# Decaying q on GpSimd so that the state's share of the output accumulates in PSUM, with the banks dealt anew and k's third buffer given up

## The chip, the core and the metric

The kernel runs on one NeuronCore of one Trainium2 chip. A core has five engines that run side by side, each with a queue of its own: TensorE (PE, with its weight loads shown apart as PEld), VectorE (DVE), ScalarE (ACT), GpSimd (POOL) and SyncE (SP, which here issues the transfers). They work on the on-chip memory SBUF; PE writes its sums to a second memory, PSUM, which this program divides into eight banks: two `pj`, two `a`, two `b`, one `c`, one `d`. The metric is the device time of one execution in microseconds (us), the median of some runs.

## What is computed

Two residual layers and a final RMS norm over 1024 tokens of width 1024: an even layer (dilated attention beside a gated recurrence) and an odd layer (gated delta rule). Only the odd layer is touched. Its core, per value head, cut to what matters:

```python
attn_qk = jnp.einsum('bhnid,bhnjd->bhnij', qc, kc) * decay
q_dec = qc * jnp.exp(gcum)[..., None]
k_tail = kc * jnp.exp(gcum[..., -1:] - gcum)[..., None]
g_last = jnp.exp(gcum[..., -1])

def step(state, inp):
    u_n, w_n, a_n, qd_n, kt_n, gl_n = inp
    v_new = u_n - jnp.einsum('bhcd,bhdv->bhcv', w_n, state)
    o = jnp.einsum('bhcd,bhdv->bhcv', qd_n, state) + jnp.einsum('bhij,bhjv->bhiv', a_n, v_new)
    new_state = state * gl_n[..., None, None] + jnp.einsum('bhcd,bhcv->bhdv', kt_n, v_new)
    return new_state, o
```

`q` and `k` come out of a projection, a causal convolution over four tokens and SiLU, and are normalised; `v` likewise without the norm. Sixteen value heads share eight key heads, two to one. The output `o` is the sum of two parts: the decayed `q` against the state of the chunks before, and the chunk's own attention against its new values.

## The kernel before

The odd layer works through eight key heads, `hh` 0 to 7, with two value heads `e` each. The 1024 tokens are eight chunks of 128. For each head there are four pieces of work, written as Python generators, each `yield` giving a number that says how much other work is to be written behind it.

- `proj(j)` is filling work for PE. From head 2 on it first writes `way_out(j-2)`, the gate projection `oz` in four halves of 24 matmuls; then `conv` for k of head j+1, for the two value heads of head j (`v..0`, `v..1`), and for q of head j, each in two halves of 512 tokens and 24 matmuls (lines 143 to 145). A half's sums go from one of two `pj` banks by ACT into `ub`, which has one buffer (line 822); ACT writes the first product into the destination tile (line 825), DVE adds three (line 827), ACT takes tanh into `ub` (line 830) and DVE finishes (line 831). The destination of k is `kT`, from `k_tile`, with three buffers; that of q is `q`, with two; that of a value head is `cv`, with one.
- `invert(hh)` inverts the lower triangular matrices of head hh: `kk` into bank `c` (line 986), a long chain on DVE (lines 1004 to 1009), and small matmuls from bank `c` in turn, `qp`, `up`, `q2`, `u2` (lines 1030 to 1061).
- `recur(hh)` walks the eight chunks. For chunk c: `ks` = k against the state (line 1105, bank `b`), `r` on DVE (line 1108), `qs` = q against the state (line 1111, bank `d`), its decay by ACT into `oq` (line 1114), `vp` (line 1120, bank `d`), `vt` on DVE and `vn` on ACT from it, `kv` (line 1129, bank `b`), the new state `S` on DVE (line 1133), `op` = attention against `vn` (line 1140, bank `b`), the next chunk's `qk` (line 1091, bank `d`), and on DVE the sum of `op` and `oq` into `bv` (line 1143), which ACT squares (line 1148). Bank `d` has one buffer, `b` two. `decay_a(c)` loads the decays of a chunk into `gca`, GpSimd adds the causal mask (line 1079) and ACT takes two exponentials (line 1081); this is done one chunk ahead.
- `normed` and `gated` finish a head: GpSimd scales `bv` (line 928), PE transposes it (line 935).

The three loops are woven together while the program is written: `mix(recur(hh), fill, 2.8)` with `fill = blend(invert(hh+1), proj(hh+1), 0.8)`. So while head hh is in its recurrence, head hh+1 is inverted and k of head hh+2 is convolved. Going through the numbers that the generators yield, from head 2 on the four `oz` halves are written by chunk 2, k's two halves beside chunk 4's `ks` and `vp`, the first value head's halves beside chunk 5 and chunk 6's `ks`, the second value head's beside chunks 6 and 7, and q's at the end.

The written order is a priority, not the order in the queues: the tile framework deals the instructions to the engines when it builds the program, a tile's first write waiting until the slot it takes has been given up by its last reader. What is then in an engine's queue runs in that order. The attention of the even layer alone has PE's order fixed by hand.

At the last head the filling work is the output projection; `y_parts(0)` takes two `kT` slots and two of `kn` for its first operands.

Of the kernel before, what the change touches and what calls it, by code (L numbers as in the profile page):

```python
# [9 lines left out]
F32 = mybir.dt.float32  # L10
F32R = mybir.dt.float32r
BF16 = mybir.dt.bfloat16
I32 = mybir.dt.int32
AF = mybir.ActivationFunctionType
ALU = mybir.AluOpType
# [3 lines left out]
P = 128  # L19
D = 1024  # L20
T = 1024
# [57 lines left out]
def trunk_kernel(ctx: ExitStack, tc: tile.TileContext, x, ew, ewo, ow, owab, owo, nw, fnw, lbl, hnw,  # L79
                 cw, dtb, alog, onw, cst, out):  # L80
    nc = tc.nc
    dve, act, pe, pool = nc.vector, nc.scalar, nc.tensor, nc.gpsimd
# [8 lines left out]
    def bank(tag, shape, name):  # L91
        return pp.tile(shape, F32, name=name, tag=tag, bufs=BANKS[tag])
# [647 lines left out]
    def odd_layer(es):  # L740
        sp = es.enter_context(tc.tile_pool(name="od", bufs=1))
        gt = {n: sp.tile([P, NT, 16], F32, name=f"g_{n}") for n in ("beta", "gc", "ngc", "eg", "nbeg", "etl", "egl")}
# [70 lines left out]
        KT, KN, SC, Q, BV, CQ, SS, VT, US = {}, {}, {}, {}, {}, {}, {}, {}, {}  # L813
# [32 lines left out]


        def k_tile(j):
            KT[j] = sp.tile([P, T], F32, name=f"kT{j}", tag="kT", bufs=3)
            return KT[j]  # L850

        def q_tile(j):
# [108 lines left out]
        def decays(hh, c, w):  # L961
            g = sp.tile([P, 2, 128], F32, name=f"gc{w}{hh}_{c}", tag=f"gc{w}", bufs=2)
            nc.sync.dma_start(g, bass.AP(tensor=gcd.tensor, offset=gcd.offset + (c * 16 + 2 * hh) * 128,
                                         ap=[[0, P], [128, 2], [1, 128]]))
            return g

        def invert(hh):
            kT = KT[hh]
# [4 lines left out]
            def decay_l(c):  # L973
                gcB = decays(hh, c, "l")

                for e in range(2):
                    act.activation(gcB[:, e, :], gcB[:, e, :], AF.Relu, bias=gt["ngc"][:, c, 2 * hh + e:2 * hh + e + 1])
                act.activation(gcB, gcB, AF.Exp, scale=-1.0)
                return gcB

            ahead_l = [decay_l(0)]
            for h in range(2):
                kk = bank("c", [P, 4, 128], f"kk{hh}_{h}")
                for c in range(4 * h, 4 * h + 4):
                    k_ = kT[:, c * 128:(c + 1) * 128]
                    pe.matmul(kk[:, c - 4 * h, :], k_, k_, start=True, stop=True)
                for c in range(4 * h, 4 * h + 4):
                    gcB = ahead_l.pop()
                    if c < NT - 1:
                        ahead_l.append(decay_l(c + 1))  # L990
                    for e in range(2):
                        dve.scalar_tensor_tensor(L[:, 2 * c + e, :], kk[:, c - 4 * h, :], SC[hh][:, 0, c, e:e + 1],
                                                 gcB[:, e, :], op0=ALU.mult, op1=ALU.mult)
                yield (15 if h else 7.0), 0.9


            for b in range(4):
# [32 lines left out]
                    pe.matmul(qp[a0[r], u, :], L[b0[r], u, a0[r]], Un[b0[r], u, :], start=True, stop=True)  # L1030
            act.copy(Q_[a0[0], :, 0:32], qp[a0[0]])
            dve.tensor_copy(Q_[a0[1], :, 0:32], qp[a0[1]])
            yield 1.5, 1.3
            up = bank("c", [P, 16, 32], f"up{hh}")
            for u in range(16):
                for r in range(2):
# [8 lines left out]
                r = slice(32 * b, 32 * b + 32)  # L1045
                pool.tensor_copy(U[r, :, r], Un[r])

            yield 2.0, 1.8
            for h in range(2):

                q2 = bank("c", [P, 4, 64], f"q2{hh}_{h}")
                for u in range(8 * h, 8 * h + 8):
                    pe.matmul(q2[u % 2 * 64:u % 2 * 64 + 64, u // 2 % 4, :], L[64:128, u, 0:64], U[64:128, u, 64:128],
                              start=True, stop=True)
# [3 lines left out]
            for h in range(2):  # L1058
# [3 lines left out]
                for e in range(2):  # L1062
                    d = U[0:64, 8 * h + e:8 * h + 8:2, 64:128]
# [8 lines left out]
        def recur(hh):  # L1072

            kT, kn, q, bv, U = KT[hh], KN[hh], Q[hh], BV[hh], US[hh]
            ss = SS[hh] = sp.tile([P, NT, 2], F32, name=f"oss{hh}", tag="oss", bufs=2)

            def decay_a(c):
                DA = decays(hh, c, "a")
                pool.tensor_tensor(DA, DA, MA[:, None, :].to_broadcast([P, 2, 128]), op=ALU.add)
                for e in range(2):  # L1080
                    act.activation(DA[:, e, :], DA[:, e, :], AF.Exp, bias=gt["ngc"][:, c, 2 * hh + e:2 * hh + e + 1])
                return DA

            def attend(c):

                DA = ahead_a.pop()
                if c < NT - 1:
                    ahead_a.append(decay_a(c + 1))
                qk = bank("d", [P, 128], f"qk{hh}_{c}")
                s = slice(c * 128, (c + 1) * 128)  # L1090
                pe.matmul(qk, kT[:, s], q[:, s], start=True, stop=True)
                A = sp.tile([P, 2, 128], F32, name=f"A{hh}_{c}", tag="A", bufs=2)
                dve.tensor_tensor(A, qk[:, None, :].to_broadcast([P, 2, 128]), DA, op=ALU.mult)
                return A

            ahead_a = [decay_a(0)]
            yield 1.0
            A = attend(0)
            St = None
            for c in range(NT):  # L1100
                col = [slice(2 * hh + e, 2 * hh + e + 1) for e in range(2)]
                s = slice(c * 128, (c + 1) * 128)
                if c:
                    ks = bank("b", [P, 2, 128], f"ks{hh}_{c}")
                    pe.matmul(ks, kT[:, s], St, start=True, stop=True)
                    r_ = sp.tile([P, 2, 128], F32, name=f"r{hh}_{c}", tag="r")
                    for e in range(2):
                        dve.scalar_tensor_tensor(r_[:, e, :], ks[:, e, :], SC[hh][:, 1, c, e:e + 1],
                                                 bv[:, c, e, :], op0=ALU.mult, op1=ALU.add)
                    qs = bank("d", [P, 2, 128], f"qs{hh}_{c}")  # L1110
                    pe.matmul(qs, q[:, s], St, start=True, stop=True)
                    oq = sp.tile([P, 2, 128], F32, name=f"oq{hh}_{c}", tag="oq")
                    for e in range(2):
                        act.activation(oq[:, e, :], qs[:, e, :], AF.Copy, scale=gt["eg"][:, c, col[e]])
                else:
                    r_ = bv[:, 0]
                yield 1.0
                vp = bank("d", [P, 2, 128], f"vp{hh}_{c}")
                for e in range(2):
                    pe.matmul(vp[:, e, :], U[:, 2 * c + e, :], r_[:, e, :], start=True, stop=True)  # L1120
                if c < NT - 1:
                    vt = sp.tile([P, 2, 128], F32, name=f"vt{hh}_{c}", tag="vt")
                    dve.tensor_tensor(vt, vp, gt["etl"][:, c, 2 * hh:2 * hh + 2, None].to_broadcast([P, 2, 128]), op=ALU.mult)
                vn = sp.tile([P, 2, 128], F32, name=f"vn{hh}_{c}", tag="vn")
                act.copy(vn, vp)
                yield 1.0
                if c < NT - 1:
                    kv = bank("b", [P, 2, 128], f"kv{hh}_{c}")
                    pe.matmul(kv, kn[:, c, :], vt, start=True, stop=True)
                    Sn = sp.tile([P, 2, 128], F32, name=f"S{hh}_{c}", tag="S", bufs=2)  # L1130
                    if c:
                        for e in range(2):
                            dve.scalar_tensor_tensor(Sn[:, e, :], St[:, e, :], gt["egl"][:, c, col[e]],
                                                     kv[:, e, :], op0=ALU.mult, op1=ALU.add)
                    else:
                        dve.tensor_copy(Sn, kv)
                    St = Sn
                op = bank("b", [P, 2, 128], f"op{hh}_{c}")
                for e in range(2):
                    pe.matmul(op[:, e, :], A[:, e, :], vn[:, e, :], start=True, stop=True)  # L1140
                A = attend(c + 1) if c < NT - 1 else None
                if c:
                    dve.tensor_tensor(bv[:, c], op, oq, op=ALU.add)
                else:
                    dve.tensor_copy(bv[:, c], op)
                for e in range(2):
                    jk = sp.tile([P, 128], BF16, name=f"oj{hh}_{c}_{e}", tag="jk", bufs=2)
                    act.activation(jk, bv[:, c, e, :], AF.Square, accum_out=ss[:, c, e:e + 1])
                yield 1.0
# [8 lines left out]
        def y_parts(g):  # L1158
            if g:
                return y_load(*y_tile(f"lo{g % 2}", 8 + g), g * 256)  # L1160
            yh = [sp.tile([P, T], F32R, name=f"oyh{c}", tag="kT", bufs=3) for c in range(2)]
            yl = [sp.tile([P, T], F32R, name=f"oyl{c}", tag="kn", bufs=3) for c in range(2)]
            y_load(yh, yl, 0)
            for t in range(NT):
                nc.sync.dma_start(hres(t), h1[t * 128:(t + 1) * 128, :])
            return yh, yl
# [103 lines left out]
```

## Time and profile before

| what | us |
|---|---|
| median of three runs | 2290.05 (2288.1 to 2291.62) |
| the profiled execution, its own time | 2290.27 |
| its span, first to last instruction | 2288.5 |
| recurrence, first `ks` to last `ks` | 1342.5 to 2122.2 |
| PE busy from 1340 to 2045, sum of the rows of the windows | 644 of 705 |
| DVE busy in the same stretch | 556 |
| ACT busy in the same stretch | 394 |

A row of a group names the line, the engine, the operation, the output and inputs by the program's names, the count, then the busy time and the mean of one in ns, then the engine's idle time ahead of them and who ended it. A row of the waits names who waited for whom, the sum in us, how often, and the longest. A matmul on float32 appears as two instructions. In the windows each engine's busy time in a stretch is followed by its count of instructions. Matmul ends are modelled and some records are missing, so PE's busy time is a guide and the distance from one start to the next is the better measure of its pace.

### The profile page before, as it was taken

What the parts mean: (1) busy time and instruction counts of PE and PEld (TensorE: products, weight loads), DVE (VectorE), ACT (ScalarE), POOL (GpSimd) and SP (SyncE); (2) the same over time, 40 slices, a digit from 0 to 9 for tenths busy, and PEclk for the clock granted to TensorE, in tenths of its full rate; (3) what the DMA queues carried; (4) which work ended last, traced back from release to release, by engine and by line L of the source; (5) the groups of instructions that cost most, each with busy time, mean ns of one, the idle gap of its engine ahead of it and who ended that gap; (6) DMA issues with size and microseconds to landing.
All of it is one profiled execution on the core that took longest, in us unless ns stands there. A gap on an engine that the chain in (4) does not pass through costs nothing. (4 is left out here: it accounts for less than half of the span.)

```text
span 2288.5 us, 54642 instructions
## 1 busy us (share of the span) xinstructions
PE 2171.9 (95%) x22597; PEld 1809.0 (79%) x22597; DVE 1427.0 (62%) x3364; ACT 963.4 (42%) x2623; POOL 226.5 (10%) x236
## 2 busy tenths in 40 slices
PE   7999999999999999988999988989899989899998
PEld 6888888898888888866887776767777767678787
DVE  6444444444444444456777887878788877855777
ACT  5333333333333332322236663755555555544223
POOL 0000000000000000000000012131212121210000
PEclk9999999999999999999999998999999999999999
DMA  4111111113222323352323221121212121214232
GB/s 145 38 48 48 44 47 48 43 39 95 78 82 84 90 83 92 97 160 88 102 97 104 59 56 62 53 79 46 76 43 76 52 74 59 65 60 148 91 113 109
DMA packets 101864, 175.83 MB, mean 77 GB/s; under 512 B 16752, under 2 KB 34032, under 8 KB 101616
## 3 DMA queue, kind: packets, MB, share of 16 engines
q1 hardware_dynamic: 101616, 172.35, 24.2%
q8 instruction: 177, 2.90, 0.5%
q14 instruction: 71, 0.58, 0.1%
HBM read 127.07 MB, written 25.23 MB: 67 GB/s over the span
## 5 line engine op out<-in xcount | busy, mean ns | idle before, releaser
L113 DVE TENSOR_TENSOR w_lo<-raww,w_hi 128x512 fp32r<-128x512 f32 x292 | 211.9, 727 | 151.1 <-ACT w_hi L112 147.1
L112 ACT CAST w_hi<-raww 128x512 fp32r<-128x512 f32 x292 | 181.1, 620 | 270.1 <-PE op L145 68.0
L143 PE MATMUL av<-w_hi,hn_hi 128*128 128x256 f32 x512 | 149.0, 291 | 0.0
L143 PE MATMUL bi<-w_hi,hn_hi 128*128 128x256 f32 x512 | 147.0, 287 | 0.0
L144 PE MATMUL bi<-w_lo,hn_hi 128*128 128x256 f32 x512 | 145.3, 284 | 0.0
L144 PE MATMUL av<-w_lo,hn_hi 128*128 128x256 f32 x512 | 144.8, 283 | 0.0
L145 PE MATMUL bi<-w_hi,hn_lo 128*128 128x256 f32 x512 | 144.8, 283 | 0.0
L145 PE MATMUL av<-w_hi,hn_lo 128*128 128x256 f32 x512 | 144.7, 283 | 0.0
L575 ACT ACTIVATE P<-P,nm 128x256 f32<-128x256 f32 (+7 forms) x128 | 71.4, 559 | 130.2 <-DVE nm L573 130.0
L143 PE MATMUL op<-w_hi,yplo 128*128 128x512 f32 x288 | 113.5, 394 | 1.6 <-DVE hr L273 0.9
L145 PE MATMUL op<-w_hi,yplo 128*128 128x512 f32 x288 | 112.2, 390 | 0.0
L144 PE MATMUL op<-w_lo,yplo 128*128 128x512 f32 x288 | 112.1, 389 | 0.0
L143 PE MATMUL pv<-hn_hi,w_hi 128*128 128x512 f32 x256 | 107.0, 418 | 2.6 <-ACT uv L822 2.6
L143 PE MATMUL oz<-hn_hi,w_hi 128*128 128x512 f32 x256 | 109.4, 427 | 0.0
L273 DVE TENSOR_TENSOR hr<-hr,op 128x512 f32<-128x512 f32 x128 | 86.1, 684 | 34.5 <-PE op L145 34.0
L145 PE MATMUL pv<-hn_hi,w_lo 128*128 128x512 f32 x256 | 104.3, 407 | 0.0
L144 PE MATMUL pv<-hn_lo,w_hi 128*128 128x512 f32 x256 | 102.6, 401 | 0.0
L144 PE MATMUL oz<-hn_lo,w_hi 128*128 128x512 f32 x256 | 102.3, 400 | 0.0
L145 PE MATMUL oz<-hn_hi,w_lo 128*128 128x512 f32 x256 | 102.0, 398 | 0.0
L581 DVE STREAM_TRANSPOSE PB<-P 128x256 f32<-128x256 f32 (+3 forms) x64 | 54.6, 854 | 74.9 <-ACT P L575 74.8
L143 PEld LDWEIGHTS av<-w_hi,hn_hi 128*128 128x128 f32 x512 | 97.9, 191 | 3.5 <-issue 1.9
L144 PEld LDWEIGHTS bi<-w_lo,hn_hi 128*128 128x128 f32 x512 | 98.1, 192 | 0.0
(354 smaller groups left out, 6044.9 us busy)
## 6 DMA issues: line engine op xcount, KB each, us to landing
raww<-in_ew_dram SPq DMA_DIRECT2D x128, 256.0 KB, 3.1
raww<-in_ow_dram SPq DMA_DIRECT2D x100, 256.0 KB, 3.0
V<-v SPq DMA_DIRECT2D x256, 64.0 KB, 2.0
rawy<-ymix SPq DMA_DIRECT2D x64, 256.0 KB, 2.7
raww<-in_ewo_dram SPq DMA_DIRECT2D x32, 256.0 KB, 3.0
gcl<-gcd SPq DMA_DIRECT2D x64, 128.0 KB, 3.0
gca<-gcd SPq DMA_DIRECT2D x64, 128.0 KB, 3.0
ymix<-oy SPq DMA_DIRECT2D x32, 256.0 KB, 2.0
```

Source lines behind the costliest of these rows:

```text
L112: act.copy(hi, raw)
L113: dve.tensor_tensor(lo, raw, hi.bitcast(F32), op=ALU.subtract)
L143: pe.matmul(ps, lh, rh, start=start, stop=False)
L144: pe.matmul(ps, lh, rl, start=False, stop=False)
L145: pe.matmul(ps, ll, rh, start=False, stop=stop)
L273: dve.tensor_tensor(dst[:, n], src[:, n], ps, op=ALU.add)
L575: act.activation(Pm[:, e, w0:], Pm[:, e, w0:], AF.Exp, bias=nmx[:, e:e + 1], scale=0.125, accum_out=den[:, i, e:e + 1])
L581: dve.transpose(PB[:, :, i * WG + w0:(i + 1) * WG], Pm[:, :, w0:])
```

## The change

- `decay_a(c)` also makes, from chunk 1 on, `qe`: ACT takes the exponential of the raw decays for both value heads in one instruction of 128x256, and GpSimd multiplies it with q. This stands ahead of the mask's addition on the same tile. `qe` has two buffers of 1 KB per partition.
- `qs`, `oq` and the two ACT instructions of line 1114 are gone. In their place the bank of `op` is opened at that point by two matmuls per chunk, `qe` of each value head against its state, and the attention's matmuls add to it later. ACT copies the finished `op` to `bv` (also in chunk 0), where DVE had added or copied.
- Banks: `op` now alone in `d`; `ks`, `vp`, `kv` and `qk` in turn in the two buffers of `b`.
- `kT` has two buffers instead of three. The last head's `y_parts(0)` takes one slot of `kT` and one of `q`.
- Three yields of `invert` ask for more filling work behind them: 9.0 instead of 7.0 after the first `kk`, 3.0 instead of 1.5 after `qp`, 4.0 instead of 2.0 after `up`.

```diff
         def k_tile(j):
-            KT[j] = sp.tile([P, T], F32, name=f"kT{j}", tag="kT", bufs=3)
+            KT[j] = sp.tile([P, T], F32, name=f"kT{j}", tag="kT", bufs=2)
...
-                yield (15 if h else 7.0), 0.9
+                yield (15 if h else 9.0), 0.9
...
-            yield 1.5, 1.3
+            yield 3.0, 1.3
...
-            yield 2.0, 1.8
+            yield 4.0, 1.8
...
                 DA = decays(hh, c, "a")
+                if c:
+
+                    qe = QE[c] = sp.tile([P, 2, 128], F32, name=f"qe{hh}_{c}", tag="qe", bufs=2)
+                    act.activation(qe, DA, AF.Exp)
+                    pool.tensor_tensor(qe, qe, q[:, None, c * 128:(c + 1) * 128].to_broadcast([P, 2, 128]), op=ALU.mult)
                 pool.tensor_tensor(DA, DA, MA[:, None, :].to_broadcast([P, 2, 128]), op=ALU.add)
...
-                qk = bank("d", [P, 128], f"qk{hh}_{c}")
+                qk = bank("b", [P, 128], f"qk{hh}_{c}")
...
-                    qs = bank("d", [P, 2, 128], f"qs{hh}_{c}")
-                    pe.matmul(qs, q[:, s], St, start=True, stop=True)
-                    oq = sp.tile([P, 2, 128], F32, name=f"oq{hh}_{c}", tag="oq")
+
+                    op = bank("d", [P, 2, 128], f"op{hh}_{c}")
+                    qe = QE.pop(c)
                     for e in range(2):
-                        act.activation(oq[:, e, :], qs[:, e, :], AF.Copy, scale=gt["eg"][:, c, col[e]])
+                        pe.matmul(op[:, e, :], qe[:, e, :], St[:, e, :], start=e == 0, stop=False, skip_group_check=True)
...
-                vp = bank("d", [P, 2, 128], f"vp{hh}_{c}")
+                vp = bank("b", [P, 2, 128], f"vp{hh}_{c}")
...
-                op = bank("b", [P, 2, 128], f"op{hh}_{c}")
+                if not c:
+                    op = bank("d", [P, 2, 128], f"op{hh}_{c}")
                 for e in range(2):
-                    pe.matmul(op[:, e, :], A[:, e, :], vn[:, e, :], start=True, stop=True)
+                    pe.matmul(op[:, e, :], A[:, e, :], vn[:, e, :], start=not c and e == 0, stop=True, skip_group_check=True)
                 A = attend(c + 1) if c < NT - 1 else None
-                if c:
-                    dve.tensor_tensor(bv[:, c], op, oq, op=ALU.add)
-                else:
-                    dve.tensor_copy(bv[:, c], op)
+                act.copy(bv[:, c], op)
...
-            yh = [sp.tile([P, T], F32R, name=f"oyh{c}", tag="kT", bufs=3) for c in range(2)]
+            yh = [sp.tile([P, T], F32R, name=f"oyh{c}", tag=t, bufs=2) for c, t in enumerate(("kT", "q"))]
```

More of the change, by code (lines that the diff above doesn't have):

```diff
@@ L1094, in attend @@
                 return A
+            QE = {}
             ahead_a = [decay_a(0)]
```

## The prediction, as put on record before the change was run

> **What bounds the kernel now.** First the page's busy times, then the windows of one head's round, then PE's waits. The change lies in the odd layer alone, from 1225 us on.
>
> ```profile
> PE 2171.9 (95%) x22597; PEld 1809.0 (79%) x22597; DVE 1427.0 (62%) x3364; ACT 963.4 (42%) x2623; POOL 226.5 (10%) x236
> ...
> 1511.30:1553.90 42.60, 36.45 (x207) 29.60 (x206) 28.01 (x81) 27.43 (x93) 9.11 (x10) 1.00 0.27 87
> 1553.90:1595.50 41.60, 39.22 (x392) 31.25 (x391) 38.96 (x109) 22.13 (x66) 6.59 (x9) 1.00 0.13 40
> 1595.50:1617.80 22.30, 22.30 (x114) 18.61 (x113) 16.79 (x39) 10.56 (x27) 6.49 (x5) 1.00 0.21 64
> ...
> PE op L1140 <- ACT vn L1125: 12.1, 15, 1.5
> PE vp L1120 <- ACT oq L1114: 8.8, 10, 1.7
> PE ks L1105 <- DVE S L1133: 8.7, 7, 1.8
> PE ot L935 <- POOL bv L928: 5.7, 7, 3.1
> PE kk L986 <- DVE L L992: 5.5, 4, 1.5
> PE q L1053 <- ACT L L1041: 4.9, 6, 2.1
> PE vp L1120 <- DVE r L1108: 3.9, 4, 1.0
> PE up L1037 <- DVE Q L1032: 3.1, 4, 1.2
> ```
>
> The three windows (length, then busy us of PE, PEld, DVE, ACT, POOL) are one round, from the first `vp` of head 2 to that of head 3: 106.5 us. PE is idle for 6.15 us of the first, 2.4 of the second and nothing of the third. PE sets the pace while it has work; DVE comes next (39 of 41.6 us in the second). What can be gained is PE's idle time, and the waits name it: over 1340 to 2140 us, 8.8 us for `oq`, 12.1 for `vn`, 8.7 for the state, and 5.5, 4.9 and 3.1 at three places of the inversion. So an edit pays only where it ends one of these waits, or costs where it starves PE.
>
> **Part 1: the opening matmuls.** Two matmuls of 128x256 columns in all (`qs`, as x2) become four instructions of half the width.
>
> ```profile
> 1518.13 0.60 PE L1105 MATMUL ks<-S,kT 128*128 128x256 f32 x2
> ...
> 1518.57 0.59 PE L1111 MATMUL qs<-S,q 128*128 128x256 f32 x2
> ...
> 1528.03 0.61 PE L1140 MATMUL op<-vn,A 128*128 128x128 f32 x4
> ...
> 1528.47 0.39 PE L1091 MATMUL qk<-q,kT 128*128 128x128 f32 x2
> ```
>
> In PE's timeline from start to start, x2 of the wide form takes 0.44 us and x4 of the narrow form 0.44 too. Cost on PE: nothing, 56 times over.
>
> **Part 2: DVE, ACT, POOL.**
>
> ```profile
> L1143 DVE TENSOR_TENSOR bv<-op,oq 128x256 f32<-128x256 f32 x56 | 23.3, 417 | 1.5 <-PE op L1140 1.5
> ...
> L1114 ACT ACTIVATE oq<-qs,g_eg 128x128 f32<-128x128 f32 x112 | 34.6, 357 | 7.3 <-PE qs L1111 7.0
> L978 ACT ACTIVATE gcl<-gcl 128x256 f32<-128x256 f32 x64 | 26.2, 410 | 0.6
> L1125 ACT COPY vn<-vp 128x256 f32<-128x256 f32 x64 | 23.4, 366 | 22.8 <-DVE vt L1123 18.3 <-PE vp L1120 2.9 <-DVE uq L818 1.1
> ...
> L1079 POOL TENSOR_TENSOR gca<-gca,MA 128x256 f32<-128x256 f32 x64 | 49.6, 775 | 459.2 <-DMA gca<-gcd 265.0 <-DVE Tp L1009 63.7 <-ACT jtq L843 39.7
> ```
>
> DVE loses 23.3 us, and 8 copies of about the same kind. ACT loses 34.6 and gains 64 copies like `vn` (23.4) and 56 exponentials like L978 (56 x 0.41 = 23.0): 11.8 us more, on an engine busy for 394 of 705 us between 1340 and 2045. POOL gains 56 x 0.775 = 43 us beside 142. None of the three is on the path: the windows show PE ahead of all. Their cover is the chunk of lead that `decay_a` has; `qe` and the mask together take 0.41 + 0.775 + 0.775 + 0.8 = 2.8 us behind a transfer, while `ks` follows `ks` at 9 to 18 us in this round. I cost it at nothing. If the cover went, the opening matmul would stand in PE's queue and everything behind it, up to one POOL instruction (0.78 us) for each of 56 chunks; and from the other side, 26 us less on DVE could shorten waits on DVE by as much as the 8.7 us of the state. I take zero.
>
> **Part 3: banks.** `vp` no longer waits for the bank that `oq` has to empty; the 8.8 us go. What is then last ahead of `vp` is `r` (3.9 us of waits today, already counted beside it). `op` now waits for ACT's copy of the `op` before, which is some ten us old by then: nothing. `qk` shares `b` with `vp`, whose readers `vt` and `vn` are done ahead of `op` anyway. **-8.8 us** (bounds 0 and -12.7, with `r`'s).
>
> **Part 4: wider distances.** They stand behind the first `kk`, behind `qp` and behind `up`, where PE waits 5.5, 3.1 and 4.9 us. More filling work there can take all of it, 13.5, or none, since the order is dealt anew. I take half, **-6.8 us**.
>
> **Part 5: k's third buffer.** This is the term that decides. While head hh is in its recurrence, k of hh+2 is convolved, and k of hh+1 is being inverted: three tiles are alive. With two buffers the first write of the new tile (L825) must wait until the last `ks` of the recurrence has read the old one.
>
> ```profile
> 1553.89 0.78 ACT L825 ACTIVATE kT<-uk,cws 128x512 f32<-128x512 f32 x1
> ...
> 1595.48 0.59 PE L1105 MATMUL ks<-S,kT 128*128 128x256 f32 x2
> ...
> L827 DVE SCALAR_TENSOR_TENSOR kT<-uk,cws,kT x6: 743/746/748, 1555.1 to 1562.8; 128x512 f32<-128x512 f32 x6
> L825 ACT ACTIVATE kT<-uk,cws x2: 724/753/782, 1553.9 to 1559.9; 128x512 f32<-128x512 f32 x2
> L830 ACT ACTIVATE uk<-kT x2: 625/628/631, 1558.5 to 1563.7; 128x512 f32<-128x512 f32 x2
> L831 DVE SCALAR_TENSOR_TENSOR kT<-uk,kT x2: 682/683/684, 1559.9 to 1564.6; 128x512 f32<-128x512 f32 x2
> ...
> L145 PE MATMUL pv<-hn_hi,w_lo 128*128 128x512 f32 x30 | 12.7, 422 | 0.0
> ...
> L145 PE MATMUL pk<-hn_hi,w_lo 128*128 128x512 f32 x6 | 2.3, 392 | 0.0
> ```
>
> In this round the write stands at 1553.9 and that `ks` at 1595.5: 41.6 us too early. The write is moved behind it, and with it a queue of others: `ub` has one buffer, so the first value head's sums can't leave the two `pj` banks, and PE's filling work ends with them. (On ACT itself nothing stands behind the write: the recurrence's own `vn` copies run there, so the order dealt must put the write behind them.)
>
> How much is blocked? From 1553.9 to 1595.5 PE did the end of k's conv and 90 `pv` matmuls (the two L145 rows of that window, times three lines). Each value head has 48, so 42 belong to the second: at 0.23 us from start to start 9.7 us, with the transposes `tk` and `tv` some 11 us that can no longer run there. The rest, 30 us, suffices for the recurrence up to about chunk 6, as the yields write it; the rest of chunk 6 runs with no cover. One round of the chain is `ks` 0.44, `r` 2 x 0.34, `vp` 0.44, `vt` 0.42, `kv` 0.44, `S` 2 x 0.34 and `ks` 0.44, 3.5 us, and about 4.1 with six hand-overs of 0.1. PE's own work in it is 2.2 us: **1.9 idle**.
>
> Then the release. Up to the moment in which `ub` is free again, both halves of k go through: 0.75 (L825), 2 x 3 x 0.746 on DVE, 2 x 0.68 (the tanh of each lies beside DVE's other half), then 0.58 for ACT to empty a `pj` bank: 7.2 us, 7.5 with hand-overs. Beside it PE has `vp` and `op` of the last chunk and k's transposes, 0.44 + 0.44 + 0.9: **5.7 idle**. Together 7.6 us a head. From the other side: nothing, if PE still has filling work at the release; 12 if DVE, with four conv halves to catch up (12 x 0.75 + 4 x 0.68 = 11.7 us in place of 5.9), lets the second value head wait as well.
>
> Six k tiles wait, those of heads 2 to 7. The last five stand in a round like this one: 5 x 7.6 = 38. The first differs.
>
> ```profile
> 1302.00:1338.00 36.00, 32.91 (x339) 26.19 (x338) 33.81 (x90) 17.49 (x45) 4.74 (x7) 1.00 0.15 45
> 1338.00:1390.00 52.00, 46.33 (x257) 37.31 (x256) 42.61 (x123) 34.05 (x106) 4.95 (x7) 1.00 0.24 58
> 1390.00:1422.00 32.00, 26.05 (x289) 19.39 (x288) 21.90 (x56) 10.89 (x24) 14.67 (x16) 0.79 0.17 55
> ```
>
> Head 2's k is convolved from 1302 on today, before head 0's recurrence begins at 1338, so it would wait until about 1338 + 8 x 4.2 = 1371; then 7.5 us, and four blocked halves of 24 matmuls (22 us) with transposes, to 1403. That is 19 us ahead of today's 1422, but without the four `oz` halves, 22 us: 3 us lost, with up to 16 if DVE slows the chain to 6 us a chunk. I take 5. **+43 us** for this part, bounds 0 and 76.
>
> The sum: 43 - 8.8 - 6.8 = +27.4. The profiled execution took 2290.3 us (span 2288.5 and 1.8 around it), the median is 2290.05, so both give the same: **2318 us**.
>
> **A rule beside it.** DVE and POOL touch each other in this trace:
>
> ```profile
> L1079 POOL TENSOR_TENSOR gca<-gca,MA x64: 721/737/1721, 1259.3 to 2105.7; 128x256 f32<-128x256 f32 x64
> ...
> L827 DVE SCALAR_TENSOR_TENSOR vT<-uv,cws,vT x96: 700/748/1240, 1266.4 to 2020.3; 128x512 f32<-128x512 f32 x96
> ```
>
> Both have a longest instance far over the median (1721 against 737 ns, 1240 against 748). The Trainium skill, SBUF — State Buffer, section "Who interferes with whom", says that a DVE instruction with two SBUF inputs contends with a GpSimd instruction that reads SBUF; L827 and the inversion's chain are of that kind. It speaks against new GpSimd work. The outliers agree with it; by it alone part 2 would not be free, and the sum would be that of rival C.
>
> **Rivals.**
>
> A, the forecast: 2318, own range 2300 to 2340.
>
> B, not slower: the wait for `kT` is hidden. If the order dealt lets the recurrence run ahead of the written one, so that its last `ks` comes before PE has used up the 48 matmuls of the first value head, then the release costs nothing and parts 3 and 4 remain: 2290 - 15.6, up to the whole 22.3 and the state's 8.7, so 2259 to 2275; 2270. For it: the chain needs 4.1 us a chunk and takes 6 to 18, and in the first window PE has 6 us of idle time for it. Against it: the filling work is written ahead of the later chunks, and the trace follows the written order closely (k's first write between chunk 4's `ks` and `vp`, as written). It decides at 11 us: by so much the recurrence must come forward.
>
> C, more: the new POOL work meets DVE's instructions as in the longest row of L827, each meeting costing up to 1240 - 748 = 0.49 us, 56 x 0.49 = 27 us on a DVE that is the next bound: 2345. For it the 39 of 41.6 us; against it that k's and the value head's conv leave just that window.
>
> D, the same: the wait costs some 3 us a head and the gains pay for it: 2290.
>
> **How the numbers follow.** Chances: A 0.50, B 0.25, C 0.15, D 0.10. Forecast 2318. The range takes in B's lower end and the upper bound of the wait (76 with part of the gains): 2262 to 2368. Faster by over 0.2% (which is about what a measurement can tell from none): 0.25; within 0.2%: 0.10; slower: 0.65.
>
> **What would show it.** Right: k's L825 starts behind the last `ks` in each head, PE's idle time is gathered in one gap of 5 us or more behind that, and waits on DVE or ACT of the conv stand ahead of `pv`. Part 3: no wait of `vp` on ACT; part 4: less at `kk`, `up` and `q2`. Wrong: L825 ahead of that gap's end with PE busy through it (B); L827 and `tm` longer in the mean (C). What would upset the sum most is a dealt order far from the written one.

## The result and the profile after

The changed kernel takes 2391.6 us (median of four runs, 2384.7 to 2399.1) against 2289.1 for the kernel before: a ratio of 1.0447, with a 95% interval of 1.0413 to 1.0480. It is 102 us slower; the forecast was 28 us slower, with 2368 as the top of its range. The profiled execution is the slowest of the four: 2399.1 us, span 2397.3.

First the busy times on the page of the changed kernel.

```profile
span 2397.3 us, 54902 instructions
## 1 busy us (share of the span) xinstructions
PE 2214.4 (92%) x22709; PEld 1846.5 (77%) x22709; DVE 1442.0 (60%) x3300; ACT 974.1 (41%) x2631; POOL 259.2 (11%) x292
```

The span grew by 108.8 us (2397.3 - 2288.5). PE is idle for 182.9 us of the span (2397.3 - 2214.4) where it was 116.6 (2288.5 - 2171.9): 66.3 us are **waiting**. The other 42.5 us are **longer matmuls**: PE's busy time rose from 2171.9 to 2214.4, though the 112 instructions more are two halves each of 56 wide ones and bring no columns. The prediction had a term for the first of these and none for the second. The second is the granted clock. In short windows the trace shows it at 1.00 or at 0.50 (below); the same matmul of L143 is 0.39 us long at 1623.59 us and 0.80 at 1640.12, in a stretch at 0.50. Added up over the stretches at 0.50, PE is busy for 24 us in the kernel before and 103 in the changed one, and half of the difference, 40 us, is nearly all of the 42.5.

Where it sits is seen by rounds. The windows below run from the first `vp` of a head to that of the next (length, then busy PE, PEld, DVE, ACT and POOL, then the granted clock), ahead of head 0, for heads 0 to 6, and from head 7 on. First the kernel before:

```profile
1225.00:1338.20 113.20, 103.21 (x691) 81.80 (x690) 91.30 (x241) 70.83 (x189) 7.31 (x10) 0.98 0.26 63
1338.20:1422.00 83.80, 72.18 (x542) 56.54 (x541) 64.51 (x178) 44.75 (x130) 19.62 (x23) 0.92 0.21 57
1422.00:1511.30 89.30, 83.29 (x618) 65.83 (x617) 74.59 (x218) 54.23 (x170) 16.93 (x20) 1.00 0.19 57
1511.30:1617.80 106.50, 97.96 (x710) 79.47 (x709) 83.76 (x227) 60.13 (x183) 22.19 (x24) 1.00 0.20 64
1617.80:1725.10 107.30, 99.64 (x701) 80.84 (x700) 85.39 (x225) 61.01 (x183) 21.35 (x24) 1.00 0.20 62
...
1941.00:2041.90 100.90, 90.27 (x643) 72.33 (x642) 75.98 (x195) 51.55 (x151) 17.46 (x21) 0.98 0.19 60
2041.90:2288.50 246.60, 236.07 (x1088) 193.94 (x1086) 158.46 (x279) 78.65 (x189) 20.35 (x20) 0.99 0.33 113
```

and the changed kernel:

```profile
1225.00:1333.40 108.40, 93.86 (x635) 73.93 (x633) 77.69 (x203) 61.46 (x162) 8.28 (x12) 0.95 0.30 66
1333.40:1432.10 98.70, 77.75 (x542) 61.30 (x543) 74.35 (x205) 51.26 (x153) 22.31 (x27) 0.86 0.14 38
1432.10:1548.30 116.20, 101.29 (x720) 82.19 (x720) 88.20 (x223) 64.63 (x192) 22.17 (x28) 0.97 0.21 60
1548.30:1673.40 125.10, 106.27 (x715) 86.62 (x714) 87.11 (x216) 62.15 (x184) 24.40 (x30) 0.95 0.18 54
1673.40:1796.90 123.50, 106.56 (x715) 86.28 (x714) 86.97 (x216) 62.34 (x184) 24.35 (x30) 0.94 0.18 54
...
2045.10:2152.30 107.20, 94.69 (x657) 76.27 (x656) 73.80 (x183) 49.78 (x142) 24.15 (x28) 0.94 0.19 53
2152.30:2397.30 245.00, 235.79 (x1101) 194.52 (x1099) 159.03 (x271) 79.86 (x189) 25.73 (x26) 0.99 0.33 114
```

The loss lies in heads 0 to 5, those whose recurrence a new k has to wait for: 14.9 us in the first, 26.9 in the second, 18.6 and 16.2 in the next two, and so on; head 6, with no new k, loses 6.3 and the last stretch nothing. Take head 3's round, 107.3 us before and 123.5 after, with the same matmuls but for 14 instructions more from the split ones. Its idle time rose from 7.7 (107.30 - 99.64) to 16.9 us, its busy time by 6.9, and its granted clock fell from 1.00 to 0.94.

Inside head 2's round, ACT's timeline around the point where that head's recurrence ends (start, duration):

```profile
1629.36 1.34 ACT L825 ACTIVATE kT<-uk,cws 128x512 f32<-128x512 f32 x2
...
1634.08 1.24 ACT L830 ACTIVATE uk<-kT 128x512 f32<-128x512 f32 x2
1636.62 0.28 ACT L843 ACTIVATE jtk<-tk 128x128 bf16<-128x128 f32 x1 [1.30 <-PE tk L840]
...
1638.98 0.60 ACT L877 COPY kn<-tk 128x512 f32<-128x512 f32 x1
1639.44 1.11 ACT L822 COPY uv<-pv 128x512 f32<-128x512 f32 x2
```

and PE's, with one matmul from ahead of it:

```profile
1623.59 0.39 PE L143 MATMUL pv<-hn_hi,w_hi 128*128 128x512 f32 x1
...
1628.65 0.67 PE L1111 MATMUL ks<-S,kT 128*128 128x256 f32 x2
...
1631.01 0.71 PE L1147 MATMUL op<-vn,A 128*128 128x128 f32 x4 [0.49 <-ACT vn L1131]
1635.47 1.11 PE L840 MATMUL tk<-ident,kT 128*128 128x128 f32 x4 [3.75 <-DVE kT L831]
...
1640.12 0.80 PE L143 MATMUL pv<-hn_hi,w_hi 128*128 128x512 f32 x1 [0.98 <-ACT uv L822]
```

k's first write (L825) stands right behind the last `ks`, as predicted. Then PE waits 3.75 us in one piece for k's convolution, does k's transposes, and takes up filling work at 1640.12 only, behind the emptying of a `pj` bank (L822). The granted clock, in windows ahead of the gap, over it and behind it, and then the stretch at 0.50 by itself:

```profile
1604.60:1629.40 24.80, 22.25 (x252) 17.75 (x251) 10.87 (x26) 9.67 (x32) 4.10 (x7) 1.00 0.16 44
1629.40:1639.00 9.60, 5.36 (x28) 4.63 (x26) 8.07 (x22) 6.95 (x31) 2.04 (x3) 0.74 0.05 16
1639.00:1654.00 15.00, 14.02 (x57) 11.32 (x57) 14.26 (x35) 6.21 (x14) 2.97 (x3) 0.82 0.09 17
...
1634.00:1644.20 10.20, 7.75 (x26) 6.60 (x27) 8.44 (x28) 6.29 (x24) 4.03 (x4) 0.50 0.01 2
1644.20:1654.00 9.80, 9.80 (x48) 8.10 (x47) 9.44 (x23) 3.41 (x7) 0.00 (x0) 1.00 0.14 27
```

The mean is 1.00 ahead of the gap, 0.74 in it and 0.82 in the 15 us behind it, when PE has work again; from 1634.0 to 1644.2 the clock is at 0.50 throughout. At five of the six gaps of this kind it stays there for 10.2 us, at the sixth for 3.4: 55 of the changed kernel's 128 us at 0.50, where the kernel before has 32. The other stretches were not followed one by one. The Trainium skill, TensorE: Matmul & The Clock Gate, section "HAM oscillation — how this bites in real kernels", gives a rule that PE should not be idle for more than some 3.4 us; the 3.75 us here, with the lower clock behind them, agree with it. They do not show that one long piece is needed: in the same round of e1 below no idle piece is over 2.5 us, and the clock is at 0.50 for 13.7 us from 1644.5 on.

Last, PE's waits between 1300 and 2260 us (total, times, longest):

```profile
PE tk L840 <- DVE kT L831: 22.4, 6, 4.4
PE op L1147 <- ACT vn L1131: 20.0, 23, 2.5
PE ks L1111 <- DVE S L1139: 16.3, 11, 2.0
PE kv L1135 <- DVE vt L1129: 12.9, 16, 1.7
PE vp L1126 <- DVE r L1114: 11.2, 12, 1.5
```

The wait of `vp` for `oq` is gone. The six waits of k's transposes are new (one of 1.1 us before), and the recurrence's own waits have all grown (`vn` from 12.1 to 20.0, `S` from 8.7 to 16.3). That fits filling work that is held up and can't cover them. It is not the whole of it: with k's buffer alone (e1) they are 17.9 and 10.6, and with the banks alone (e7) `S` is at 12.5.

### The profile page after: what moved, and what is told of

Same layout as the page of the kernel before. It is cut to its first block, busy times and chain, and to the rows that moved or that the text cites. A ratio compares the mean times of both kernels' runs of the same rounds, so it can differ in the third digit from the quotient of the medians.

```text
span 2397.3 us, 54902 instructions
## 1 busy us (share of the span) xinstructions
PE 2214.4 (92%) x22709; PEld 1846.5 (77%) x22709; DVE 1442.0 (60%) x3300; ACT 974.1 (41%) x2631; POOL 259.2 (11%) x292
## 5 line engine op out<-in xcount | busy, mean ns | idle before, releaser
L143 PE MATMUL av<-w_hi,hn_hi 128*128 128x256 f32 x512 | 149.0, 291 | 0.0
L143 PE MATMUL bi<-w_hi,hn_hi 128*128 128x256 f32 x512 | 147.0, 287 | 0.0
L143 PE MATMUL pv<-hn_hi,w_hi 128*128 128x512 f32 x256 | 111.4, 435 | 8.1 <-ACT uv L822 8.1
L143 PE MATMUL op<-w_hi,yplo 128*128 128x512 f32 x288 | 113.4, 394 | 1.6 <-DVE hr L273 0.9
L143 PE MATMUL oz<-hn_hi,w_hi 128*128 128x512 f32 x256 | 107.8, 421 | 0.0
L143 PEld LDWEIGHTS av<-w_hi,hn_hi 128*128 128x128 f32 x512 | 97.9, 191 | 3.5 <-issue 1.9
L145 PEld LDWEIGHTS av<-w_hi,hn_lo 128*128 128x128 f32 x512 | 97.9, 191 | 0.4 <-issue 0.4
```

What stands on the lines that cost most here:

```text
L143: pe.matmul(ps, lh, rh, start=start, stop=False)
L145: pe.matmul(ps, ll, rh, start=False, stop=stop)
```

## The experiments

Each ratio is to the kernel before on the same chip, with its 95% interval. The parts of the change are taken alone first, then k's wait is taken apart, then `qe`.

**e1: k's buffer alone.** The kernel before, with

```diff
-            KT[j] = sp.tile([P, T], F32, name=f"kT{j}", tag="kT", bufs=3)
+            KT[j] = sp.tile([P, T], F32, name=f"kT{j}", tag="kT", bufs=2)
...
-            yh = [sp.tile([P, T], F32R, name=f"oyh{c}", tag="kT", bufs=3) for c in range(2)]
+            yh = [sp.tile([P, T], F32R, name=f"oyh{c}", tag=t, bufs=2) for c, t in enumerate(("kT", "q"))]
```

> The kernel before with two buffers for kT instead of three (and the last head's first operands in one slot of kT and one of q), nothing else. Theory (k's third buffer makes the whole loss): five rounds of some 123 us in place of 107 and a first one later by some 15, so 2289 + 5 x 16 + 15 = 2384, between 2370 and 2405. Rival (the new wiring of q, the banks and the distances cost it, and the buffer alone costs what the prediction said): 2289 + 43 = 2332.

2402.8 us, 1.0501 (1.0482 to 1.0521): 113 us, more than the whole change.

```profile
PE 2223.6 (93%) x22597; PEld 1843.6 (77%) x22597; DVE 1447.7 (60%) x3364; ACT 964.4 (40%) x2623; POOL 215.7 (9%) x236
```

On its page PE's busy time is 51.7 us above the kernel before with the very same instructions, and the idle time (span 2400.5) 60.3 us: the same two parts as in the changed kernel. At a clock of 0.50 PE is busy for 128 us, and half of what that is above the kernel before, 52 us, is all of the longer matmuls.

**e2: the change with the third buffer back.** The room comes from the junk outputs of ACT's squares, which share one buffer here:

```diff
-            KT[j] = sp.tile([P, T], F32, name=f"kT{j}", tag="kT", bufs=2)
+            KT[j] = sp.tile([P, T], F32, name=f"kT{j}", tag="kT", bufs=3)
...
-                    jk = sp.tile([P, 128], BF16, name=f"j{name}_{h}_{c}", tag="jkq", bufs=2)
+                    jk = sp.tile([P, 128], BF16, name=f"j{name}_{h}_{c}", tag="jk", bufs=1)
...
-                    jk = sp.tile([P, 128], BF16, name=f"oj{hh}_{c}_{e}", tag="jk", bufs=2)
+                    jk = sp.tile([P, 128], BF16, name=f"oj{hh}_{c}_{e}", tag="jk", bufs=1)
...
-            yh = [sp.tile([P, T], F32R, name=f"oyh{c}", tag=t, bufs=2) for c, t in enumerate(("kT", "q"))]
+            yh = [sp.tile([P, T], F32R, name=f"oyh{c}", tag="kT", bufs=3) for c in range(2)]
```

> The changed kernel with the third buffer of kT given back; the room comes from one buffer for ACT's two kinds of throw-away squares, instead of two for each. Theory: the loss goes and the gains of the banks and the distances are left, 2289 - 16 = 2273, between 2255 and 2289. Rival (the new wiring costs): 2330 or more.

2335.7, 1.0205 (1.0188 to 1.0222). 56 us go, but 46 stay: the rest of the change costs that, in place of the gain of 16 that was expected.

**e3: the change with the old distances** (7.0, 1.5, 2.0).

> The changed kernel with the old distances in the inversion (7.0, 1.5, 2.0). Theory: the distances are a matter of some us either way, 2385 to 2400. Rival (the wider distances push the inversion into the stretch that the missing buffer has emptied): 2375 or less.

2374.2, 1.0367 (1.0349 to 1.0384): the wider distances cost 17 us in the changed kernel.

**e4: work in the gap.** The changed kernel, with nine matmuls whose result is not read behind the last chunk of heads 1 to 5:

```diff
+                if c == NT - 1 and 1 <= hh < 6:
+                    dm = bank("c", [P, 2, 128], f"dm{hh}")
+                    for _ in range(9):
+                        pe.matmul(dm, vn[:, 0, :], vn, start=True, stop=True)
```

> The changed kernel with nine matmuls of 128x256 on float32 (2 instructions each, 4 us together) that nobody reads, in heads 1 to 5, between the last op of a recurrence and k's transposes, where PE sits idle for 4 to 5 us. They do not shorten the chain. If the lower granted clock behind the gap is a part of the loss (112 us at half clock in the odd layer after the change against 21 before), those stretches shrink and the time falls by 10 to 25 us, to 2367 to 2382. If the clock only falls where PE waits anyway, the time stays within 5 us of 2392 or rises.

2380.5, 1.0405 (1.0385 to 1.0426): 11 us less in the median with more work, though the two intervals overlap. The trace is clearer than the time. The wait of `tk` on k's convolution falls from 22.4 to 5.8 us, the mean clock of the profiled execution rises from 0.973 to 0.984, and PE's busy time at 0.50 falls from 103 to 66 us, half of which is 19. The two profiled executions differ by 20.7 us, but they are the slowest of the one kernel and the fastest of the other. So the clock at the gap is a part of the loss. How large a part this does not settle, for the padding fills only some 4 of the 10 us.

**e5: both at once**, e2 with the old distances: `qe` and the banks are what is left of the change, beside the shared junk.

> The changed kernel with the third k buffer and the old distances: only q's decay on GpSimd and the banks remain. If the distances make the 46 us that were left with the buffer given back, this comes to 2280 to 2295; if they are worth the 17 us that they were with two buffers, to 2319; if the new wiring of q and the banks costs by itself, it stays over 2315.

2319.9, 1.0126 (1.0109 to 1.0143).

**e6 and e7: the distances alone, and the banks alone, on the kernel before.**

> The kernel before with the wider distances alone. Prediction's part 4: 2289 - 7, at best - 13. Rival (they push the inversion's chain on DVE later, into the values' convolutions, and starve PE): 2305 to 2320.

> The kernel before with the banks dealt as after (ks, vp, kv, qk in the two of b; qs, then op, in d), q's decay still by ACT and DVE, three k buffers, old distances. Prediction's part 3: vp no longer waits for oq, so 2289 - 9 = 2280. Rival (four tiles in two banks bind the chain's steps to one another, so each chunk's vp, kv and ks wait longer): 2300 or more.

2299.0 for both: 1.0036 (1.0020 to 1.0052) and 1.0042 (1.0027 to 1.0056). Each was to gain 7 to 9 us and costs 9. With the banks alone `vp` waits for `oq` no longer; the largest waits are now, from 1300 to 2260 us:

```profile
PE ks L1105 <- DVE S L1133: 12.5, 12, 1.8
PE op L1140 <- ACT vn L1125: 11.8, 14, 1.5
PE kk L986 <- DVE L L992: 6.3, 5, 1.6
PE kv L1129 <- DVE vt L1123: 6.2, 5, 2.5
```

`S` rose from 8.7 to 12.5 and `vt` from 1.0 to 6.2: one chain, `ks` to `ks`, waits a link later. On e7's page

```profile
PE 2178.5 (95%) x22597; PEld 1812.2 (79%) x22597; DVE 1423.0 (62%) x3364; ACT 961.6 (42%) x2623; POOL 226.2 (10%) x236
```

with a span of 2295.1, PE's idle time is the 116.6 us of the kernel before: in this execution the moved waits cancel, and the 6.6 us of loss are longer matmuls, with 41 us at a clock of 0.50 against 32. e6 is alike: 7.5 of the 9.3 us by which its span grew are busy time. There the wait of `kk` for `L` (5.5 before) is gone, and those of `vp` for `oq` and of `kv` for `vt` have risen, from 8.8 to 13.6 and from 1.0 to 6.4.

**e8: `qe` alone**, with old banks, old distances, three buffers of k and the shared junk.

> q decayed on GpSimd and summed in PSUM, with the old dealing of the banks (vp and qk in d; ks, op, kv in b), three k buffers and old distances. Part 2 of the prediction: no cost, 2289 within 10. Rival (the chain of decays on ACT, GpSimd and back is too long for the chunks' pace, or b is held by the open sum): 2305 or more.

2324.0, 1.0149 (1.0127 to 1.0171).

**e9: the shared junk alone**, the control that e2, e5 and e8 lack.

> The kernel before with the one thing that the runs with a third buffer for k had to change beside it: the junk outputs of ACT's squares share one buffer. Theory (the shared buffer costs nothing, since all its writers are on ACT, which runs them in order): 2290, within 5. Rival (the semaphore on the one buffer, or the order dealt, costs time): up to the 34 us that qe alone measured, so 2300 to 2324; then part of that 34 is this edit's.

2307.7, 1.0078 (1.0062 to 1.0094). The theory that it costs nothing falls: 18 us. `qe` itself therefore costs about 16 of e8's 34 us (2324.0 - 2307.7). On e9's page, with the instructions of the kernel before:

```profile
PE 2186.4 (95%) x22597; PEld 1819.7 (79%) x22597; DVE 1421.6 (62%) x3364; ACT 967.1 (42%) x2623; POOL 229.1 (10%) x236
```

14.5 of the 19 us by which its span grew are longer matmuls, and its clock is at 0.50 for 71 us where the kernel before has 32. All writers of the junk are on ACT; what the edit changes beside that is the order in which the builder dealt the instructions, and the traces of the two do show ACT and DVE in another order in the odd layer. Why that order has more stretches at 0.50 stays open.

**e10 to e12: what `qe` costs.** e10 multiplies on DVE, e11 leaves that on GpSimd and copies `bv` on DVE, e12 is e9 with one more GpSimd multiply per chunk and nothing else:

```diff
-                    pool.tensor_tensor(qe, qe, q[:, None, c * 128:(c + 1) * 128].to_broadcast([P, 2, 128]), op=ALU.mult)
+                    dve.tensor_tensor(qe, qe, q[:, None, c * 128:(c + 1) * 128].to_broadcast([P, 2, 128]), op=ALU.mult)
...
-                act.copy(bv[:, c], op)
+                dve.tensor_copy(bv[:, c], op)
...
+                if c:
+                    gq = sp.tile([P, 2, 128], F32, name=f"gq{hh}_{c}", tag="gq", bufs=1)
+                    pool.tensor_tensor(gq, DA, q[:, None, c * 128:(c + 1) * 128].to_broadcast([P, 2, 128]), op=ALU.mult)
```

> qe alone (old banks, old distances, three buffers of k), its multiply put on DVE, GpSimd left as before. Theory G (GpSimd's work slows DVE, or its 0.77 us stand in the way): the 34 us of qe alone shrink although DVE now does 56 multiplies of 0.42 us (23 us, as much as the bv adds that went): 2295 to 2310, and the convolution's L827 back at a mean of 0.76 us from 0.84. Rival H (ACT's new work, the exponential and the copy of bv ahead of vn, or the four matmuls of op held behind the state): as slow as with GpSimd or slower, 2320 to 2335.

> qe alone, its multiply on GpSimd, but the copy of the output chunk out of PSUM on DVE, where the add stood before, in place of ACT. Theory H (ACT is too late in the recurrence: its copy stands ahead of vn and of the bank's release): a good part of the 34 us goes, 2295 to 2312, and the waits of ks on the copy and of op on vn shrink from 4.0 and 14.1 us. Rival G (GpSimd beside DVE): no gain, 2320 to 2335, since DVE is given 23 us more.

> The kernel before (with the shared junk buffer) and 56 further GpSimd multiplies of a decay tile by q, as qe's, into a tile that nobody reads; nothing else moves. Theory G: GpSimd's work alone costs 56 meetings of up to 0.5 us with DVE, 10 to 27 us: 2300 to 2317, L827's mean up from 0.76 to 0.83 us. Rival H: 2290, within 5, with L827's mean as before or its growth hidden.

2316.4 (1.0120, 1.0105 to 1.0135), 2321.1 (1.0136, 1.0119 to 1.0153) and 2333.9 (1.0195, 1.0180 to 1.0210). e10 and e11 have e8 for their control and overlap with it; e10 lies between what its two theories expected. Only e12 stands clear of its control, e9: 26 us for work that nothing waits for. Its page:

```profile
PE 2193.0 (94%) x22597; PEld 1822.7 (78%) x22597; DVE 1437.0 (62%) x3364; ACT 968.7 (42%) x2623; POOL 272.7 (12%) x292
```

GpSimd is busy 43.6 us longer than in e9, and DVE 15.4 us longer (1437.0 - 1421.6) with the same 3364 instructions. Taken one by one, DVE's instructions that run beside one of GpSimd are longer than the median of their own shape by 41.5 us in sum in e9 and by 55.1 in e12. That is the meeting of the two engines that rival C described. What the prediction cited from the Trainium skill, SBUF — State Buffer, section "Who interferes with whom", agrees with it. The lengthening is not where e12's expectation looked for it: the mean of L827 on `vT` is 770 ns in e9 and 765 in e12. Nor need all 26 us come from it, since ACT and DVE run in another order here too, and another order alone came with 18 us in e9. Whether GpSimd, ACT's new work or the `b` bank that `op` holds from its opening on is what `qe` costs in e8 is not settled.

**e13: k's wait kept, the blocking behind it taken away.** e1 with

```diff
-            ub = sp.tile([P, T + 3], F32, name=f"u{name}", tag="ub")
+            ub = sp.tile([P, T + 3], F32, name=f"u{name}", tag="ub", bufs=2)
...
-        nwf = sp.tile([P, D], F32, name="nwf", tag="ub")
+        nwf = sp.tile([P, D], F32, name="nwf", tag="ub", bufs=2)
```

> The kernel before with two buffers for k (as in e1, which took 2402.8) and two for ub, so that the first value head's sums can leave the pj banks while k's write still waits for the last ks. Theory U (the prediction's chain: ub's one buffer carries k's wait to the filling work): the recurrence gets some 11 us more fill per head and the gap behind it shrinks, so half or more of the 113 us goes: 2320 to 2350. Rival K (it is k's own write with what stands behind it, the convolution's halves on DVE and the half clock after the gap): little changes, 2385 to 2405, and the rounds stay near 123 us.

2308.6, 1.0078 (1.0057 to 1.0099): **94 of the 113 us are gone**, at one more buffer elsewhere. Around the end of a recurrence, first e1's windows, then e13's (each stretch is the 25 us ahead of k's first write, the 10 us behind it, and 15 more):

```profile
1617.00:1642.00 25.00, 20.23 (x133) 15.25 (x134) 8.48 (x22) 7.80 (x24) 1.96 (x3) 0.86 0.09 27
1642.00:1652.00 10.00, 5.56 (x23) 4.57 (x24) 8.61 (x23) 6.25 (x26) 1.23 (x1) 0.62 0.04 13
1652.00:1667.00 15.00, 14.03 (x58) 11.26 (x57) 13.59 (x34) 6.61 (x17) 4.04 (x4) 0.80 0.05 14
```

```profile
1584.00:1609.00 25.00, 25.00 (x214) 20.41 (x205) 15.03 (x31) 11.84 (x31) 1.25 (x2) 1.00 0.11 33
1609.00:1619.00 10.00, 9.85 (x52) 7.82 (x51) 7.98 (x16) 8.09 (x32) 0.74 (x1) 1.00 0.17 54
1619.00:1634.00 15.00, 15.00 (x79) 12.35 (x78) 14.54 (x38) 7.77 (x15) 0.00 (x0) 1.00 0.00 0
```

ACT's timeline of e13 shows that k still waits for the last `ks`:

```profile
1608.96 1.34 ACT L825 ACTIVATE kT<-uk,cws 128x512 f32<-128x512 f32 x2 [1.43 <-PE ks L1105]
```

So k's wait by itself costs little. It is the filling work queued behind it through `ub` that costs: with a second `ub`, PE has a value head's more of it (some 11 us by the prediction's count), works through the 10 us behind k's write, and the clock stays at 1.00. In e1 133 instructions of PE fall into the last 25 us of the recurrence, in e13 214. What a second `ub` does beside three buffers of k was not run; if it helps there too, a part of the 94 us is that gain.

**e14 and e15: the same instructions, other distances.** e14 is narrower (5.5, 1.0, 1.5), e15 has 7.2 for 7.0.

> The kernel before with the three distances narrower instead of wider (5.5, 1.0, 1.5 for 7.0, 1.5, 2.0). Theory O (a newly dealt order costs by itself, whichever way the distances go, since the waits it makes are not those that the builder counted): 2295 to 2310. Rival W (the distances work as named, and wider is what costs): 2275 to 2288, faster than before.

> The kernel before with one distance 7.2 in place of 7.0, which moves few instructions (some 60 on PE). Theory O: between 0 and +15 us without any mechanism to name, so 2290 to 2305. Rival: 2290, within 3, since next to nothing is moved.

2294.8, 1.0019 (1.0006 to 1.0032), and 2289.2, 0.9996 (0.9986 to 1.0006). Wider costs 9 us, narrower 4, a trifle nothing. A small new deal of the order, as e15's, is thus not a loss by itself; but the kernel before sits at or near the best of the distances tried.

**e16 and e17: the second `ub` in the changed kernel**, with new and with old distances (for room, shared junk and one buffer for q's sums of squares, which has no control).

> The changed kernel, two buffers for k as it has, and two for ub (to make room, the junk squares share one buffer and q's sums of squares have one). Theory U: what the chain through ub costs goes here too; left are qe (16 us), the shared junk (18), banks and distances (9 each, 17 for the distances in e3): 2315 to 2345. Rival (in the changed kernel the loss is its recurrence's, with its later r, S and vn): 2360 to 2390.

> As e16, with the old distances. Theory: some 10 to 17 us less than e16, as with a third buffer for k (e2 to e5: 16 us), so 2300 to 2335, and near e5's 2320. Rival: no less than e16, if the distances cost only beside a waiting k.

2338.6, 1.0214 (1.0199 to 1.0229), and 2320.9, 1.0131 (1.0113 to 1.0149). The second `ub` does in the changed kernel what a third k does (e2 2335.7, e5 2319.9): 53 us go, with two buffers of k.

No version tried beats the kernel before.

## Why the prediction was wrong

The sign was right and its reason too: k's first write moves behind the last `ks`, `ub` carries the wait to the value heads, and PE runs out of work. The forecast was +28 us and the change cost 102, nearly four times that. Its terms in order:

- **Part 1, nothing.** No run speaks against it; it was not measured by itself.
- **Part 2, nothing** (bounds -8.7 and +44). `qe` alone costs 16 us beside its control (e8, e9). The step that failed is the claim that an engine off the path is covered: GpSimd's 44 us of new work in e12 need nobody to wait for them, and DVE's instructions beside them are longer. Rival C's mechanism is thus real; its 27 us were to be lost on DVE, where e12 shows 15.4, so that the 26 us of the kernel come so close is luck, and a part of them may be the order. Which of its parts makes `qe` cost 16 stays open.
- **Part 3, -8.8.** The wait it named is gone, the time is not: +9 alone (e7). The step that failed is to book a vanished wait as time gained. What was late next was not `r` alone but the whole ring `ks`, `r`, `vp`, `vt`, `kv`, `S`: PE's idle time in e7 is what it was.
- **Part 4, -6.8.** +9 on the kernel before (e6), +17 in the changed kernel (e3). The wait at `kk` did go in e6, but `oq` and `vt` rose by more. My reading, not tried by itself: filling work put behind one yield is missing at another, so that both directions cost (e14).
- **Part 5, +43.** The deciding term, and the step on which the forecast failed: mis-sized, 113 alone (e1), of which 94 go when `ub` no longer blocks (e13). The five rounds at 7.6 us each, 38 together, lost 26.9, 18.6, 16.2, 16.4 and 15.9 in the changed kernel, 94 together. In the gap itself the estimate held: it gave 5.7 us idle at the release, and the window from 1629.4 to 1639.0 has 4.2 (9.60 - 5.36) with 0.98 more ahead of `pv`; it gave 1.9 for the tail of the recurrence, and the window before has 2.55. Three things were left out. **The clock and the lengthened matmuls:** 51.7 of 112 us in e1, 42.5 of 108.8 in the changed kernel, with PE at half clock for 128 and 103 us where it was 24; one of the prediction's own rows, 1390 to 1422 us at a granted clock of 0.79, showed that such stretches exist, and it was read for its length only. **The rest of the round:** idle time rose by 9.2 us in head 3's round, not by 7.6, as the recurrence's waits grew. **The first heads:** put at 5 us for head 0 and, as in the later rounds, 7.6 for head 1, while the two together lost 41.8, of which 4.8 had been gained ahead of them. The time of head 2's k was forecast nearly right, about 1371 (its first write stands at 1301.9 us in ACT's timeline before and at 1376.9 after); what followed from a k 75 us later was not. Why head 1 loses more than any other, 26.9, was not followed.

The terms don't add. Measured alone they are 113, 9, 9 and 16, together 147; the change costs 102. Taken off the changed kernel they are 53 to 56 for what k blocks (e16, e2) and 16 to 18 for the distances (e3; e2 to e5; e16 to e17); about 30 are left for `qe` with the banks (e5, e17), in kernels that bear the shared junk as well. How those 30 divide between `qe`, the banks and the junk stays open, and so does why a shared junk buffer costs 18 us in e9: most of it is time at half clock, but that the dealt order makes it was argued, not shown.

The range does not quite follow from what the prediction says of it: 2290 + 76 is 2366 before any gain is taken off, and it has 2368.

Of the rivals, B (the wait hidden) did not come: it decided at 11 us of recurrence brought forward, and just that much filling work, given through a second `ub`, brings nearly all back. C came in part, and D's gains did not come.

## What to carry to other kernels

When a tile loses a buffer, follow the wait to the next single buffer behind it: the cost is the filling work that stands there, and one more buffer at that place can buy back most of it (here 94 of 113 us). Look at the granted clock beside the idle time: here a stretch at half clock went with each such gap, and over the kernel the matmuls grew by 42.5 us beside 66.3 us of idle time. And a wait that vanishes from the list is a gain only if the chain it stood in has slack at the next link, so that an edit that removes one is still to be timed alone, against a control with every helping edit in it.

## What the runs showed of the hardware

In the round shown, the granted clock fell to 0.50 in a gap with one idle piece of 3.75 us, stayed there for 10.2 us, most of them with PE at work again, and then stood at 1.00; with the gap filled (e13) the corresponding windows show 1.00 throughout. In e1's round it fell to 0.50 for 13.7 us without an idle piece over 2.5 us. GpSimd's 56 multiplies of 128x256, unread and awaited by nobody, took 43.6 us of GpSimd; DVE's unchanged instructions were busy for 15.4 us more and the kernel took 26 us more, in an order that was dealt anew.
